# An inference step of a hybrid attention layer: the first weights' splits placed behind the key products, and one output weight split a stage later

## Chip, cores and metric

The kernel runs on one core of a Trainium2 chip. The metric is the device time in microseconds of one execution. A core has five engines that run side by side, each through its own program in order: TensorE (PE, matrix products; PEld is its loading of weights), VectorE (DVE), ScalarE (ACT), GpSimd (POOL) and SyncE (SP), which here issues the DMA transfers. They wait for each other on semaphores.

## The reference

One layer works on 512 prompt tokens and 64 sample tokens with a cache of 128 positions. A norm and one input projection feed two kinds of attention; their outputs go through one output projection, then through a gated feed-forward part with a short convolution and a last norm.

```
h = rmsnorm(x, g_attn)
proj = h @ w_in
q_d, k_d = rope(proj[..q..], pos), rope(proj[..k..], pos)      # differential heads
v_d = proj[..v..]
c_q, c_kv = rmsnorm(proj[..cq..], g_qa), rmsnorm(proj[..ckv..], g_kva)
k_r = rope(proj[..kr..], pos)                                  # latent heads' shared key
q_m = c_q @ w_qb;  kv = c_kv @ w_kvb
mix = concat(diff_attention(q_d, k_d, v_d), mla_attention(q_m, kv, k_r))
x1 = x + mix @ w_out
u, g = split(rmsnorm(x1, g_ffn) @ w_up)
y = x1 + (silu(causal_conv(g)) * u) @ w_down;  return rmsnorm(y, g_final), new keys, values, ...
```

## The kernel before

The 576 tokens (512 and 64) lie along the free side of the tiles, features along the 128 partitions. Columns are worked in two groups, 256 and 320 wide (GRP). A product in full precision is made of three matrix products of rounded halves: high by high, high by low, low by high (mm3, L140 to L142). So each weight tile must be split before its use: ScalarE copies the raw tile into its high half (split_hi, L126, rows named wv00h, wo0h), VectorE subtracts that from the raw one for the low half (split_lo, through tt, L84, rows named wv00l, wo0l). A weight of 1,024 columns is split in two parts of 512.

The order of work up to the feed-forward part is the order in which the program is written; it is made by generators that take steps beside each other. Two places matter here.

**The start.** TensorE makes the first pair of key products (kacc), then the first pair of query products (qacc, two halves of two column groups, 24 products each), then the values of the first heads (pv, function values, L440 to L443), then scores S (L500). Between each two inner steps of the query products, go advances two chains. first_chain does the first norm: norm_steps makes the root of the mean square for each token (r_col, GpSimd), waits ROW_STEPS steps, spreads it over the partitions (rbc, a transpose on TensorE, copied by ScalarE to r_bc, L331) and multiplies it into the rotary tables (cosr, sinr on VectorE). held_pair then multiplies the key products with the tables (pr, rope_evac, VectorE), sums them on GpSimd (st, rotate, through tt at L84 too) and stores them (store_pair, L393 and L395): eight stores of 32 rows bring the rotated rows into qkT. first_weights waits FIRST_WEIGHTS steps and then takes eight half splits, one at each step: high and low of both parts of wv00 and of wv01.

```
yield FIRST_WEIGHTS
for _ in range(8):
    filler.split()
    yield 1
```

**The filler.** Attention blocks alternate with projections that a Filler hands out in pieces. Its stages are, in order, V0, V1, ..., CQ, CKV, KR, QU, U0, U1, VM, ..., W0 (output projection). QU makes the latent queries (qracc, rotated sums q, split into qr) with the split of the shared key (kr, kro) and of the latent (lc into lat) beside it; U0 and U1 make the keys (knacc; knp, knl, kns) and queries (qnacc; qn, qnl, qns) of latent heads 0 and 1. wo0 is the first tile of the output weight. While a stage runs, its next weights are split, one half at every SPLIT_EVERY-th step, but only the weights that AHEAD lists for the stage; where it lists nothing, the weights of the next stage that has any:

```
if self.todo and self.todo[0][0] in self.ahead and self.count % SPLIT_EVERY.get(self.name, 1) == 0:
    self.split()
```

Loads of raw tiles go through SyncE's one queue, in order, with the stores; a raw buffer is loaded again when the split of the weight in it is done, so a load's place in the queue follows the split's place in the program.

Of the kernel before, what the change touches and what calls it, by code (L numbers as in the profile page):

```python
# [38 lines left out]

GAPS = ((1.0, 1.0, 1.0), (1.2, 1.2, 1.2), (0.8, 1.2, 1.2), (0.9, 0.9, 0.9), (0.8, 1.1, 1.1), (0.9, 1.0, 0.9))  # L40
NORM_STEPS = (3, 1, 4, 2)
LATE_STEPS, ROPE_STEPS, KEY_STEPS, ROW_STEPS, FIRST_WEIGHTS = 10, 2, 4, 3, 3
SPLIT_EVERY = {"V1": 3, "U1": 2, "CQ": 2, "KR": 2, "QU": 2, "U0": 2}
AHEAD = {"CQ": ("wi10", "wkr"), "CKV": ("wqr", "wqn"), "KR": ("wkv",), "QU": ("wo0",), "U0": ("wo0",)}
SQUARES_BEHIND, ADDS_BEHIND, NORM_BEGIN = 2, 3, 4
N2_FINISH, N2_SPREAD = 2, 4
Y_FINISH, Y_SPREAD, Y_CUTS = 1, 3, (0, 3, 6, 8)
# [18 lines left out]
def stream_step(ctx: ExitStack, tc: tile.TileContext, i, o):  # L66
# [887 lines left out]
    class Filler:  # L954
# [43 lines left out]
        def step(self):  # L998
# [4 lines left out]
            if self.gen is None:  # L1003
# [15 lines left out]
                self.ahead = self.loaded[first + len(specs):first + len(specs) + after]  # L1019
                if self.name in AHEAD:  # L1020
                    self.ahead = [w for w in self.loaded if w.name in AHEAD[self.name]]
                if self.name == "U1":
# [625 lines left out]
```

## Time and profile before

| | before |
|---|---|
| runs | 676.8, 675.14, 676.6 us; median 676.6 |
| profiled execution: own time | 676.81 us |
| its span in the trace | 674.9 us |
| granted TensorE clock, mean | 0.994 |
| TensorE busy | 656.8 us, 97% of the span, 4830 instructions |
| VectorE busy | 508.1 us, 75% |
| ScalarE busy | 313.8 us, 46% |
| GpSimd busy | 114.8 us, 17% |

The span is what the profile shows of the execution from its first to its last instruction; the execution's own time is 1.9 us longer. A busy share is a mean over the whole span and does not tell which engine a stage waits for; that is read from the rows' last column, in brackets, which gives an engine's idle time ahead of an instruction and who ended it.

### The profile page before, as it was taken

The page shows a single profiled execution, that of the slowest core. Times are in us where ns is not written, and L with a number is a line of the kernel's source. Part 1 is how long each engine was busy: PE and PEld are TensorE (multiplying, and loading weights), DVE is VectorE, ACT ScalarE, POOL GpSimd, SP SyncE. Part 2 cuts the span into 40 slices and gives each one's busy share as a digit, 9 for nine tenths or more (in the row PEclk, how much of TensorE's full clock was granted, in tenths as well). Part 3 has the DMA queues.
Part 4 walks back from the last instruction along what each step waited for, and adds up shares of the span by engine and source line. Part 5 has one row for each costly group of instructions (what it writes and reads, how often), then busy time and mean ns, then how long its engine had stood idle before and what let it go on. Part 6 is the DMA issues. An engine that isn't in the chain of part 4 may idle for free.

```text
span 674.9 us, 12335 instructions
## 1 busy us (share of the span) xinstructions
PE 656.8 (97%) x4830; PEld 631.5 (94%) x4830; DVE 508.1 (75%) x1022; ACT 313.8 (46%) x621; POOL 114.8 (17%) x166
## 2 busy tenths in 40 slices
PE   8999999998899999999999999999999999999995
PEld 8998897887799899999999999999999999999995
DVE  5758866778577757899999849984885788697634
ACT  8423335534634336375574236532641553464253
POOL 0131210015200016232230101210110010011042
PEclk9999999999999999999999999999999999999998
DMA  8464422225114113003133303330331133024103
GB/s 315 158 185 130 133 66 68 69 64 181 50 32 146 44 32 126 1 14 112 64 126 125 126 1 124 127 116 10 120 129 65 48 110 126 26 85 143 32 1 141
DMA packets 26249, 63.62 MB, mean 94 GB/s; under 512 B 3280, under 2 KB 6288, under 8 KB 26192
## 3 DMA queue, kind: packets, MB, share of 16 engines
q1 hardware_dynamic: 25904, 62.58, 28.3%
q8 instruction: 38, 0.62, 0.4%
q10 hardware_dynamic: 288, 0.26, 0.1%
q14 instruction: 19, 0.16, 0.1%
HBM read 55.27 MB, written 5.21 MB: 90 GB/s over the span
## 4 chain that ended last, share of the span: by engine, by line
PE 82%; DVE 10%; ACT 3%; issue 2%; DMA 1%; POOL 0%; SPq 0%; DVEq 0%; POOLq 0%; ACTq 0%
PE yacc L140 10%; PE yacc L141 9%; PE yacc L142 9%; PE ua L1265 6%; PE ua L1263 6%; PE ua L1264 6%; PE ub L1265 3%; PE ub L1264 3%; PE ub L1263 3%; PE uc L1265 2%; PE uc L1264 2%; PE uc L1263 2%; PE pv L440 2%; PE pv L441 1%; PE uplain L140 1%
## 5 line engine op out<-in xcount | busy, mean ns | idle before, releaser
L84 DVE TENSOR_TENSOR x<-x,yacc 128x288 f32<-128x288 f32 (+2 forms) x128 | 56.4, 449 | 48.8 <-PE yacc L142 48.5
L140 PE MATMUL yacc<-act,wd 128*128 128x288 f32 x288 | 85.2, 296 | 0.0
L142 PE MATMUL yacc<-act,wd 128*128 128x288 f32 x288 | 85.1, 296 | 0.0
L141 PE MATMUL yacc<-act,wd 128*128 128x288 f32 x288 | 85.1, 295 | 0.0
L141 PEld LDWEIGHTS yacc<-act,wd 128*128 128x128 f32 x288 | 54.3, 189 | 0.0
L142 PEld LDWEIGHTS yacc<-act,wd 128*128 128x128 f32 x288 | 54.3, 188 | 0.0
L140 PEld LDWEIGHTS yacc<-act,wd 128*128 128x128 f32 x288 | 54.3, 189 | 0.0
L1291 POOL COPY cst<-G 128x2 f32<-128x2 f32 x22 | 19.5, 889 | 163.7 <-DVE G L84 147.8
L468 ACT ACTIVATE p<-S,nmax 128x128 f32<-128x128 f32 (+4 forms) x36 | 18.5, 515 | 43.0 <-DVE nmax L466 42.6
L1352 ACT COPY u<-ua 128x288 f32<-128x288 f32 x20 | 8.0, 399 | 63.8 <-PE ua L1265 63.8
L87 DVE SCALAR_TENSOR_TENSOR conv<-G,vec,conv 128x578 f32<-128x578 f32 x44 | 35.8, 815 | 2.0 <-ACT conv L1296 1.9
L1278 POOL COPY G<-zero 128x2 f32<-128x2 f32 x22 | 14.4, 653 | 131.4 <-DVE conv L87 115.8
L84 POOL TENSOR_TENSOR n<-n,nsq 128x288 f32<-128x288 f32 x13 | 12.3, 950 | 75.5 <-ACT nsq L882 75.3
L1296 ACT ACTIVATE conv<-G,vec 128x578 f32<-128x578 f32 x22 | 19.2, 872 | 9.1 <-DVE G L84 9.0
L468 ACT ACTIVATE p<-Sm,nmax 128x128 f32<-128x128 f32 (+4 forms) x18 | 9.3, 515 | 28.5 <-DVE nmax L466 28.5
L84 POOL TENSOR_TENSOR st<-pr 128x256 f32<-128x256 f32 (+1 forms) x16 | 13.4, 858 | 50.0 <-DVE c L516 24.0
L90 ACT CAST act<-conv 128x576 fp32r<-128x576 f32 x22 | 14.9, 676 | 12.6 <-DVE conv L84 12.5
L1300 ACT ACTIVATE silu<-conv 128x578 f32<-128x578 f32 x22 | 15.1, 688 | 11.8 <-DVE conv L87 11.8
L480 DVE COPY pT<-tp 128x128 f32<-128x128 f32 (+3 forms) x36 | 16.6, 462 | 4.3 <-PE tp L477 3.8
L882 ACT ACTIVATE nsq<-x 128x288 f32<-128x288 f32 (+2 forms) x28 | 12.3, 443 | 16.1 <-DVE x L84 14.4
L477 PE MATMUL tp<-ident,p 128*128 128x128 f32 x84 | 15.6, 278 | 3.9 <-DVE p L795 1.3
L466 DVE TENSOR_REDUCE nmax<-S 128x1 f32<-128x128 f32 (+4 forms) x36 | 16.9, 475 | 1.1
(1585 smaller groups left out, 2536.9 us busy)
## 6 DMA issues: line engine op xcount, KB each, us to landing
qkT<-st SPq DMA_DIRECT2D x32, 72.0 KB, 2.0
xraw<-in_x SPq DMA_DIRECT2D x7, 288.0 KB, 5.8
x<-in_x SPq DMA_DIRECT2D x7, 288.0 KB, 5.9
out_y<-yo SPq DMA_DIRECT2D x4, 320.0 KB, 2.2
out_kd<-st SPq DMA_DIRECT2D x4, 288.0 KB, 2.4
out_vp<-vd SPq DMA_DIRECT2D x2, 512.0 KB, 4.2
wkr<-in_w_k SPq DMA_DIRECT2D x3, 256.0 KB, 5.4
out_y<-yo SPq DMA_DIRECT2D x2, 384.0 KB, 2.4
```

What stands on the lines that cost most here:

```text
L84: (eng or nc.vector).tensor_tensor(out=out, in0=a, in1=b, op=op)
L87: nc.vector.scalar_tensor_tensor(out=out, in0=a, scalar=s, in1=b, op0=op0, op1=op1)
L140: nc.tensor.matmul(out, lhsT=wh, rhs=xh, start=first, stop=False)
L141: nc.tensor.matmul(out, lhsT=wh, rhs=xl, start=False, stop=False)
L142: nc.tensor.matmul(out, lhsT=wl, rhs=xh, start=False, stop=last)
L466: nc.vector.tensor_reduce(out=nmax[:, 0:1], in_=Sv, axis=AX.X, op=ALU.max, negate=True)
L468: nc.scalar.activation(out=p[:, :nk], in_=Sv, func=AF.Exp, bias=nmax[:, 0:1], accum_out=sums)
L1263: nc.tensor.matmul(acc, lhsT=wh, rhs=xh, start=first and n == 0, stop=False, skip_group_check=True)
L1264: nc.tensor.matmul(acc, lhsT=wh, rhs=xl, start=False, stop=False, skip_group_check=True)
L1265: nc.tensor.matmul(acc, lhsT=wl, rhs=xh, start=False, stop=(n == len(ks) - 1), skip_group_check=True)
L1291: nc.gpsimd.tensor_copy(out=cst[:, j, 0:2], in_=G[:, 512:514])
L1296: nc.scalar.activation(out=c[:, :578], in_=G[:, 0:578], func=AF.Identity, scale=cw[0], bias=cb)
```

## The change

Four numbers change, all in the lines that set the order: the spreading of the norm's row begins after two steps instead of three, the first eight half splits after seven instead of three, and wo0 is no longer split during the stage QU. QU lists wkv, which is all split by then; U0 keeps wo0. The new entry for U1 names what U1 took by itself before.

```
-LATE_STEPS, ROPE_STEPS, KEY_STEPS, ROW_STEPS, FIRST_WEIGHTS = 10, 2, 4, 3, 3
+LATE_STEPS, ROPE_STEPS, KEY_STEPS, ROW_STEPS, FIRST_WEIGHTS = 10, 2, 4, 2, 7
 SPLIT_EVERY = {"V1": 3, "U1": 2, "CQ": 2, "KR": 2, "QU": 2, "U0": 2}
-AHEAD = {"CQ": ("wi10", "wkr"), "CKV": ("wqr", "wqn"), "KR": ("wkv",), "QU": ("wo0",), "U0": ("wo0",)}
+AHEAD = {"CQ": ("wi10", "wkr"), "CKV": ("wqr", "wqn"), "KR": ("wkv",), "QU": ("wkv",), "U0": ("wo0",), "U1": ("wkv", "wo0")}
```

On VectorE at the start, among the key products (pr from kacc) and the tables, the low halves of the first value weights move; a minus is a place of before, a plus one of the change:

```order
 L84 TENSOR_TENSOR pr<-kacc_128,cosr 128x256
 L84 TENSOR_TENSOR pr<-kacc_128,sinr 128x256
+L84 TENSOR_TENSOR wv00l<-wv00r,wv00h 128x512
 L84 TENSOR_TENSOR pr<-kacc_129,cosr 128x320
 L84 TENSOR_TENSOR pr<-kacc_129,sinr 128x320
 L84 TENSOR_TENSOR pr<-kacc_130,cosr 128x320
 L84 TENSOR_TENSOR pr<-kacc_130,sinr 128x320
-L84 TENSOR_TENSOR wv01l<-wv01r,wv01h 128x512
+L84 TENSOR_TENSOR wv00l<-wv00r,wv00h 128x512
+L84 TENSOR_TENSOR wv01l<-wv01r,wv01h 128x512 x2
```

Before, both halves of wv00l and the first of wv01l stood ahead of the tables; now one half of wv00l stands between the narrow and the wide key products, and the other three behind all of them. On TensorE the transposes rbc stand six products earlier, and ScalarE's four high halves stand behind its copies of r_bc.

On SyncE, in its queue of transfers behind the load of wi4, the first keys' stores (st to qkT, and to the output kd) change places with two loads:

```order
 L122 DMA wi4r<-in_w_in 128x512 x2
+L393 DMA qkT<-st_403 32x576 x4
+L395 DMA out_kd<-st_403 128x576
+L393 DMA qkT<-st_404 32x576 x4
+L395 DMA out_kd<-st_404 128x576
 L122 DMA wi5r<-in_w_in 128x512 x2
 L122 DMA wi6r<-in_w_in 128x512 x2
-L393 DMA qkT<-st_419 32x576 x4
```

The stores of the keys now come ahead of the loads of wi5 and wi6, which were ahead of them; the stores of the queries follow behind both, as before.

On VectorE in the stages QU and U0, around the queries' sums q and head 0's products, wo0's low halves move (the second one goes to the same place of head 1):

```order
 L87 SCALAR_TENSOR_TENSOR lc<-lc,vec,rbc 128x256
-L84 TENSOR_TENSOR wo0l<-wo0r,wo0h 128x512
 L84 TENSOR_TENSOR q<-pr 128x256
...
 L87 SCALAR_TENSOR_TENSOR pr<-qracc,msin 128x256
-L84 TENSOR_TENSOR wo0l<-wo0r,wo0h 128x512
 L84 TENSOR_TENSOR q<-pr 128x256
...
 L87 SCALAR_TENSOR_TENSOR qnl<-qnacc,qn 128x256 x2
+L84 TENSOR_TENSOR wo0l<-wo0r,wo0h 128x512
 L737 COPY kns<-knacc 128x192
```

Both low halves left QU: the first stands behind head 0's qnl, ahead of the copy kns, and the second between the two qnl of head 1. Their casts on ScalarE moved with them: the first now ahead of head 0's qn, the second ahead of head 1's knp.

## Rows read from the trace of the kernel before

**Rows 1.** TensorE's timeline, 31-37 us: start, busy us, engine, line, [idle <-releaser].
```profile
31.08 0.41 PE L140 MATMUL qacc<-xh,wq1h 128*128 128x320 f32 x1 [0.41 <-DVE pr L84]
31.33 0.31 PE L141 MATMUL qacc<-xl,wq1h 128*128 128x320 f32 x1
31.47 0.31 PE L142 MATMUL qacc<-xh,wq1l 128*128 128x320 f32 x1
...
36.97 0.28 PE L441 MATMUL pv<-wv01l,xh 128*128 128x256 f32 x1
```

**Rows 2.** VectorE's timeline, 28 to 37 us, same columns.
```profile
30.28 0.42 DVE L84 TENSOR_TENSOR pr<-kacc,cosr 128x256 f32<-128x256 f32 x1
...
32.53 0.49 DVE L84 TENSOR_TENSOR pr<-kacc,cosr 128x320 f32<-128x320 f32 x1 [0.85 <-POOL st L84]
...
34.13 0.68 DVE L84 TENSOR_TENSOR wv01l<-wv01r,wv01h 128x512 fp32r<-128x512 f32 x1
```

**Rows 3.** ScalarE's timeline, 27 to 29 us.
```profile
28.40 0.43 ACT L331 COPY r_bc<-rbc 128x320 f32<-128x320 f32 x1 [0.24 <-PE rbc L190]
```

**Rows 4.** GpSimd's timeline, 24 to 37 us.
```profile
31.76 1.43 POOL L84 TENSOR_TENSOR st<-pr 128x256 f32<-128x256 f32 x2 [5.93 <-DVE pr L84]
34.30 2.09 POOL L84 TENSOR_TENSOR st<-pr 128x320 f32<-128x320 f32 x2 [1.10 <-DVE pr L84]
```

**Rows 5.** SyncE's queue, 30 to 50 us; last, issues of 42 to 50.
```profile
34.84 0.81 SPq L122 DMA_DIRECT2D wi6r<-in_w_in  x2
35.69 2.50 SPq L393 DMA_DIRECT2D qkT<-st  x4
...
42.56 4.95 SPq L393 DMA_DIRECT2D qkT<-st  x8
...
qkT<-st SPq DMA_DIRECT2D x8, 72.0 KB, 2.1
```

**Rows 6.** TensorE's timeline, 48 us and 158 to 175 us.
```profile
48.22 0.49 PE L500 MATMUL S<-qkT 64*128 64x128 f32 x4
...
158.19 0.39 PE L140 MATMUL qracc<-lat,wqrh 128*128 128x256 f32 x1 [0.33 <-DVE pr L87]
...
163.19 0.50 PE L141 MATMUL knacc<-lat,wkvh 128*128 128x512 f32 x1 [1.32 <-DVE lat L84]
...
167.74 0.33 PE L477 MATMUL tp<-ident,p 128*128 128x128 f32 x1 [0.56 <-DVE p L87]
...
174.35 0.33 PE L477 MATMUL tp<-ident,p 128*128 128x128 f32 x1 [1.34 <-DVE p L795]
```

**Rows 7.** VectorE's timeline, 155 to 175 us.
```profile
156.00 1.39 DVE L84 TENSOR_TENSOR wo0l<-wo0r,wo0h 128x512 fp32r<-128x512 f32 x1
...
161.70 1.43 DVE L84 TENSOR_TENSOR lat<-lc,lat 128x576 fp32r<-128x576 f32 x1
...
166.13 0.42 DVE L87 SCALAR_TENSOR_TENSOR qnl<-qnacc,qn 128x256 fp32r<-128x256 f32 x1 [0.53 <-ACT qn L749]
...
170.19 0.74 DVE L87 SCALAR_TENSOR_TENSOR qnl<-qnacc,qn 128x256 fp32r<-128x256 f32 x2
```

**Rows 8.** ScalarE's timeline, 157 to 176 us.
```profile
157.56 0.61 ACT L126 CAST wo0h<-wo0r 128x512 fp32r<-128x512 f32 x1
...
159.72 0.78 ACT L694 CAST kr<-kr 64x704 fp32r<-64x704 f32 x1
...
170.96 0.22 ACT L752 ACTIVATE qns<-qnacc 128x64 f32<-128x64 f32 x1 [0.77 <-DVE qnl L87]
```

**Rows 9.** GpSimd's timeline, 148 to 195 us.
```profile
157.73 1.70 POOL L84 TENSOR_TENSOR kr<-kro,kr 64x704 fp32r<-64x704 f32 x1 [0.89 <-ACT kr L690]
161.22 2.09 POOL L84 TENSOR_TENSOR qr<-q,qr 64x512 fp32r<-64x512 f32 x2 [1.79 <-ACT qr L704]
165.77 1.70 POOL L84 TENSOR_TENSOR qr<-q,qr 64x512 fp32r<-64x512 f32 x2 [2.45 <-ACT qr L704]
```

**Rows 10.** Stretch of 2 us: engines' busy us, granted clock, DMA share, GB/s.
```profile
136.00:138.00 2.00, 2.00 (x11) 2.00 (x10) 0.00 (x0) 0.39 (x1) 0.00 (x0) 0.50 0.75 212
```

## The prediction

> **What bounds the kernel now.** I read the page's busy shares first, then the waits, then the timelines of the two stretches in which the change moves instructions. TensorE is busy for 97% of the span, so nothing off it counts unless it makes TensorE wait, and I look only at such waits. Around the first edit there is one: TensorE stands for 0.41 us at 31.08 because VectorE's first key products free their accumulator late [rows 1]. Its next matmuls follow each other by 0.14 us, but the first one holds its place for 0.25, so the stop costs about 0.5. Around the second edit there are three: 1.32 us at 163.19 for the low half of the latent, 0.56 at 167.74 and 1.34 at 174.35, both for a softmax row that VectorE finishes late [rows 6]. Behind each the chain is tight, so what makes one longer moves all that follows.
>
> The span of the profiled execution is 674.9 us and its own time 676.8, at the top of the three runs and 0.2 over their median. I sum against 676.8; about 2 us either way (0.3%) is all that a measurement can tell from no change.
>
> **First edit: tables ahead of the value weights' splits.** The transposes that spread the norm's row come out six matmuls earlier on TensorE: 6 x 0.14 = 0.9 us. In before, splits of value weights stand ahead of the table products on VectorE, the first key product starts at 30.28 [rows 2], and the second copy of the row waits for TensorE at 28.40 [rows 3]. With those transposes 0.9 earlier and no split between, the copy is done at about 28.40 + 0.43 - 0.9 = 27.9 and the second pair of tables can follow at once; four table products of about 0.37 then end near 29.0, and the first key product starts there instead of at 30.28, 1.25 earlier. TensorE's stop at 31.08 goes: **-0.5**.
>
> The three splits now come behind the key products, where GpSimd does the rotation's sums. There the rows show that the two engines do not work side by side on this kind of instruction: a low half takes VectorE 0.68 us at 34.13 [rows 2], but 1.39 at 156.00 [rows 7], while GpSimd sums the shared key; the latent's low half takes 1.43 at 161.70 [rows 7], under GpSimd's qr at 161.22 [rows 9]; and GpSimd's sums at 34.30 hold 2.09 us for two [rows 4], the first of them behind the split at 34.13. So I lay them end to end. Key products until 30.4, wv00l's half until 31.0, GpSimd's first two sums 31.0 to 32.4 (1.43, [rows 4]); VectorE's next product needs a buffer that the first of them frees, so it starts at about 31.8 (32.53 before) and four products of 0.40 end at 33.4. Then three splits of 0.6 and GpSimd's two wide sums, at 0.75 each a little over the narrow ones' 0.71, take turns: split to 34.05, sum to 34.8, split to 35.4, sum to 36.2, split to 36.9. TensorE wants that last half at 36.97 - 0.5 = 36.45 [rows 1]. It waits about 0.5: **+0.5**, and the gain of the first edit is given back. Bounds: if the splits all win their turn they are done by 35.3 and this is 0; if a sum also takes longer, 1.0.
>
> The Trainium skill, page "SBUF — State Buffer", section "SBUF: two separate sides", says that VectorE and GpSimd share a pair of ports under an exclusive lock that whoever starts first holds for a whole instruction. The 1.39 us in place of 0.68 agrees; by the page alone, without durations, one could not tell who starts first.
>
> **The queue of stores.** SyncE's list moves too. The rotated keys' stores now stand ahead of the loads of wi5 and wi6 instead of behind them. In before they start at 35.69, after the pair wi6r (0.81 from 34.84) [rows 5]; now they can start when the sums are done, and the two pairs of loads, 2 x 0.85 = 1.7 us of issuing, lie between them and the queries' stores. From the first key store to the first query store the queue needs 42.56 - 35.69 = 6.87 us, so with the first key store at 34.85 the queries' start at 34.85 + 6.87 + 1.7 = 43.4, 0.85 later. Head 0's scores need six of the eight stores: issued at 42.56 + 5/8 x 4.95 = 45.65, landed 2.1 later [rows 5], 47.75. TensorE starts those scores at 48.22 and comes to their second half at about 48.45, so 0.7 us of margin goes against 0.85 of delay: **+0.2** (0 if the sums let the keys go earlier still, 0.6 if the keys' sums end with the split at 36.2).
>
> A page puts this otherwise. The Trainium skill, "DMA: Bandwidth & Descriptors", section "Issuing engines are not separate DMA queues", calls the issuing engine's share usually small beside the transfer; by it this term would be 0 and the sum 0.2 less. The row shows 4.95 us for eight issues and 2.1 to the landing, so here the issue is the larger.
>
> **Second edit: wo0's split leaves the query stage.** It takes away two low halves on VectorE and two casts on ScalarE ahead of 163.19. Three things hold what that is worth. The half at 156.00 stood behind GpSimd anyway; the product behind it will stand there too. GpSimd's kr runs from 157.73 to 159.43 [rows 9], and VectorE's sum q(320) waits for it as before. And ScalarE's copy of kr at 159.72 [rows 8] can start only 0.25 earlier, at GpSimd's end, so GpSimd's qr comes 0.25 earlier too, at about 161.0; the latent's low half, freed of the second wo0l (0.6), is due at 161.1 and finds GpSimd there, as it does at 161.70 now. Latent 0.3 earlier: **-0.3**. Bounds: 0, and the whole 1.32 if VectorE gets in first; the two arrive 0.1 us apart, and I take the side of the rows, on which GpSimd leads.
>
> In its new place the first cast (0.61, [rows 8]) stands ahead of ScalarE's qn, and with it qnl's second half at 166.13 comes about 0.35 late. Behind it wo0l's first half is due at 166.9 less the 0.3, while GpSimd's qr (two, 1.70 us from 165.77) [rows 9], itself 0.4 later with the cast, holds it up for another 0.6; then it needs 0.6. The copy of the keys and the softmax scaling stand behind it on VectorE, and TensorE's transpose at 167.74 waits for them: 0.35 + 0.6 + 0.6 = **+1.5**. Bounds: 0.6, the half alone; 2.0, cast and the contended half of 1.39.
>
> The second cast goes ahead of head 1's knp, 0.5 after overlap, and its low half between the two qnl at 170.19 [rows 7], 0.6. ScalarE's qns at 170.96 waits for the second qnl (0.77 already) [rows 8], and the squares, qr, knp, VectorE's knl and the transpose at 174.35 stand behind in that order: 0.5 + 0.6 = **+1.1**. GpSimd is idle there, so no contention. Bounds: 0.6 if ScalarE's idle time before qn takes the cast; 1.1.
>
> Sum: -0.5 + 0.5 + 0.2 - 0.3 + 1.5 + 1.1 = +2.5; 676.8 + 2.5 = **679.3**.
>
> **The rivals.** *A, main:* 679.3, 0.4% over the median. *B, the clock:* behind a longer standstill TensorE's clock falls; in before a stretch of 2 us runs at 0.50, 1.2 GHz [rows 10], which loses 1.0 us. For it: the wait at 174.35 grows to 2.4. Against: the 1.32 and 1.34 of now leave no such stretch. 680.3. (The Trainium skill's "TensorE: Matmul & The Clock Gate", section "What's actually happening", describes a gate that lets half the pulses through when the array is not busy.) *C, the port is free:* VectorE's latent half gets in ahead of GpSimd (-1.3 for -0.3), or wo0l's first half meets no GpSimd (+0.9 for +1.5); one of them gives 678.3 to 678.7, both 677.7. That is no measurable change. For it: the two arrivals are 0.1 apart. I take 678.2. *D, nothing:* the splits land in gaps on all sides and the first gain is given back: 676.8. For it: VectorE is idle 0.53 ahead of 166.13 [rows 7]. Against: the casts use up just that gap. *E, faster:* wo0's low halves lay on TensorE's path in the query stage and lie off it in their new place. Then the wait of 1.32 at 163.19 goes whole, with it the 0.33 at 158.19 behind the contended first half [rows 6], and the 0.5 at 31.08 stays won: -2.1, 674.7. It decides at the latent's half, if that is done by 161.7, and at the transpose, if that is 1.6 earlier than 167.74. Against it stands the order on VectorE, where wo0l sits directly ahead of the softmax scaling.
>
> **How the numbers follow.** Chances: A 0.42, B 0.13, C 0.22, D 0.13, E 0.10. The likeliest is 679.3. The terms all at their lower bounds add to -0.6, 676.2, all at their upper ones to +4.2, 681.0. The range reaches down half way from D to E and up to just past B: 675.6 to 680.8. Over 678.6 counts as slower, under 674.6 as faster: slower is A and B less their lower edge, 0.50; faster E, 0.10; the same C, D and that edge, 0.40.
>
> **What would show it.** In the changed kernel's trace: no stop of TensorE ahead of the wide query products near 31; wv01l's last half at 36 to 37, interleaved with GpSimd's sums, and a wait of 0.3 to 0.7 in the first value products; query stores from about 43.4, and a wait ahead of the first scores; a wait at the latent still over 1 us near 163; wo0l's first half 1.2 to 1.4 us long near 166.6; transposes at about 169 and 176.5. It is wrong if the latent's half is done before 162 and the first wo0l takes 0.7, or if the two splits do not lie on the chain to the transposes; then the time is at 678 or below. A clock of 0.50 near 175 would point to B.

## The result and the profile after

The changed kernel takes 681.89 us (median of 4 runs, 680.67 to 682.85) against 676.36 (4 runs, 675.14 to 676.8): a ratio of 1.0087, 95% interval 1.0075 to 1.0099. It is slower, as forecast, but by 5.5 us and not 2.5, and it lies above the range.

| | before | after |
|---|---|---|
| profiled execution: own time, span | 676.81, 674.9 | 681.38, 679.5 |
| TensorE busy | 656.8 us | 658.2 us |
| VectorE busy | 508.1 us | 511.1 us |
| granted TensorE clock, mean | 0.994 | 0.990 |

I laid TensorE's instructions of both profiles side by side and read where the start of the same instruction shifts. First, rows of TensorE's timeline after, which answer to [rows 1, 6] (columns as there; in brackets at the end, the idle time ahead and who ended it):

```profile
30.54 0.31 PE L140 MATMUL qacc<-xh,wq1h 128*128 128x320 f32 x1
30.68 0.31 PE L141 MATMUL qacc<-xl,wq1h 128*128 128x320 f32 x1
...
36.53 0.38 PE L441 MATMUL pv<-wv01l,xh 128*128 128x256 f32 x1
36.75 0.28 PE L443 MATMUL pv<-wv01h,xl 128*128 128x256 f32 x1
...
50.63 0.68 PE L500 MATMUL S<-qkT 64*128 64x128 f32 x4 [2.63 <-DMA qkT<-st]
...
165.47 0.50 PE L141 MATMUL knacc<-lat,wkvh 128*128 128x512 f32 x1 [1.35 <-DVE lat L84]
...
171.28 0.33 PE L477 MATMUL tp<-ident,p 128*128 128x128 f32 x1 [1.82 <-DVE p L87]
...
179.06 0.33 PE L477 MATMUL tp<-ident,p 128*128 128x128 f32 x1 [0.98 <-DVE p L795]
```

The stop at 31.08 is gone: the same product starts at 30.54 with no idle time ahead of it, and the one behind it at 30.68 for 31.33, while the products ahead of the stop start within 0.03 us of before's: 0.7 won. The last half of wv01l, now at 36.53, costs 0.3: the product behind it starts at 36.75 for 37.10, only 0.35 earlier. Then the first scores, which started at 48.22, start at 50.63, after 2.63 us of waiting for the stores of the rotated queries. The latent's wait is 1.35, as before (1.32). The transposes wait 1.82 (0.56 before) and 0.98 (1.34). Next, SyncE's queue after, with the issues of 42 to 51 us behind it, to set beside [rows 5]:

```profile
34.67 2.50 SPq L393 DMA_DIRECT2D qkT<-st  x4
...
41.05 0.91 SPq L122 DMA_DIRECT2D wi5r<-in_w_in  x2
...
42.95 0.43 SPq L1100 DMA_DIRECT2D msin<-in_msin  x1
43.48 6.63 SPq L393 DMA_DIRECT2D qkT<-st  x8
...
qkT<-st SPq DMA_DIRECT2D x8, 72.0 KB, 4.9
```

The queries' stores start at 43.48, where the prediction had 43.4. But they take 6.63 us to issue (4.95 before), and from issue to landing 4.9 (2.1 before; both are medians of the eight). Ahead of them in the queue stand the loads of wi5, wi6 and msin: four tiles of 256 KB and one of 288 KB, issued within two and a half microseconds. Two single issues, msin and the first query store, with their time to landing, and the waits of SyncE's queue from 40.5 to 50.3 us (who waited for what: us in total, times, longest) tell more:

```profile
msin<-in_msin SPq DMA_DIRECT2D x1, 288.0 KB, 6.6
qkT<-st SPq DMA_DIRECT2D x1, 72.0 KB, 6.3
...
SPq L393 <- DMA wi6r<-in_w_in: 1.2, 2, 0.7
SPq L393 <- DMA msin<-in_msin: 0.8, 1, 0.8
```

Issued at 42.95 and 43.48, the two landed at 49.6 and 49.8: the first store came in right behind msin, and the next four 0.2 us apart, the fifth at 50.6, where TensorE's wait ends. These five were issued at the pace of before (3.06 us). The sixth to eighth were not: each was issued only when the transfer eight places ahead of it in the queue, wi6's first half, its second half and msin, had landed. That is how 4.95 became 6.63; it follows from the late landings and does not cause them. The clock, in stretches of 2 us (columns as in [rows 10]):

```profile
52.00:54.00 2.00, 2.00 (x12) 2.00 (x12) 0.97 (x3) 2.00 (x7) 0.00 (x0) 0.52 0.98 300
54.00:56.00 2.00, 2.00 (x13) 2.00 (x13) 0.43 (x2) 0.12 (x1) 0.00 (x0) 0.62 0.97 348
...
136.00:138.00 2.00, 2.00 (x21) 1.99 (x19) 1.75 (x5) 1.78 (x6) 0.66 (x2) 1.00 0.00 0
...
172.00:174.00 2.00, 2.00 (x10) 2.00 (x10) 0.76 (x2) 1.49 (x5) 0.00 (x0) 0.50 0.00 0
```

Behind the 2.63 us in which TensorE stood, the granted clock falls to the 1.2 GHz level (0.52 and 0.62 of 2.4 GHz are means of two stretches that hold some time at the full clock); behind the 1.82 us at the transpose it is 0.50. The stretch at 136, which ran at 0.50 in before [rows 10], runs at full clock. The shifts in this pair of profiles are then:

| place | predicted | measured |
|---|---|---|
| stop near 31 | -0.5 | -0.7 |
| late splits of wv00, wv01 | +0.5 | +0.3 |
| first scores, for the query stores | +0.2 | +2.8 |
| half clock behind them | 0 | +1.5 |
| half clock near 135, there in before only | 0 | -1.6 |
| query stage without wo0, read at the latent | -0.3 | -0.3 |
| first transpose | +1.5 | +1.3 |
| second transpose (from the first one to it) | +1.1 | +1.2 |

They add to 4.5 of the 4.6 us between the two profiled executions; two smaller shifts, -0.3 at a transpose near 59 us and +0.3 at one near 141, cancel.

### The profile page after: what moved, and what is told of

Same layout as the page of the kernel before. It is cut to its first block, busy times and chain, and to the rows that moved or that the text cites. A ratio compares the mean times of both kernels' runs of the same rounds, so it can differ in the third digit from the quotient of the medians.

```text
span 679.5 us, 12335 instructions
## 1 busy us (share of the span) xinstructions
PE 658.2 (97%) x4830; PEld 632.9 (93%) x4830; DVE 511.1 (75%) x1022; ACT 313.6 (46%) x621; POOL 115.8 (17%) x166
## 4 chain that ended last, share of the span: by engine, by line
PE 82%; DVE 9%; ACT 3%; issue 2%; DMA 1%; SPq 1%; POOL 1%; DVEq 0%; POOLq 0%; ACTq 0%
PE yacc L140 9%; PE yacc L141 9%; PE yacc L142 9%; PE ua L1265 6%; PE ua L1264 6%; PE ua L1263 6%; PE ub L1265 3%; PE ub L1264 3%; PE ub L1263 3%; PE uc L1265 2%; PE uc L1264 2%; PE uc L1263 2%; PE uplain L140 1%; PE tp L477 1%; PE uplain L142 1%
## 5 line engine op out<-in xcount | busy, mean ns | idle before, releaser
L477 PEld LDWEIGHTS tp<-ident,p 128*128 128x128 f32 x84 | 10.1, 140 | 8.5 <-issue 2.7
```

Source lines behind the costliest of these rows:

```text
L477: nc.tensor.transpose(out=pt_ps[:, n * P:n * P + P], in_=a[:, c:c + P], identity=ident)
```

## The experiments

Theory 1: the loads that now stand ahead of the query stores delay them as transfers, by their bytes, and not by the time that their issue takes. Rivals: the issue is what counts, as the prediction had it; the sums on GpSimd make the stores late; the loss comes from the second edit. Each kernel ran with the kernel before on the same chip; ratios are against that.

| run | what differs | median us | before us | ratio, 95% interval |
|---|---|---|---|---|
| e1_first | first edit alone | 679.39 | 676.43 | 1.0050 (1.0035 to 1.0064) |
| e2_second | second edit alone | 678.71 | 676.43 | 1.0041 (1.0026 to 1.0055) |
| e3_rows | row steps alone | 676.18 | 676.43 | 0.9994 (0.9983 to 1.0006) |
| e4_hold | change, wi6 and msin behind the stores | 680.27 | 676.43 | 1.0065 (1.0050 to 1.0080) |
| e5_behind | second edit, halves at other places of U0 | 677.22 | 676.92 | 1.0005 (0.9997 to 1.0013) |
| e6_u1 | second edit, split in U1 | 680.43 | 676.92 | 1.0060 (1.0048 to 1.0072) |
| e7_msin | row steps, msin behind the stores | 676.36 | 676.92 | 0.9996 (0.9988 to 1.0005) |
| e8_both | e7 and e5 together | 676.01 | 676.92 | 0.9987 (0.9979 to 0.9995) |
| e9_issue | e4 with three tiny transfers added | 681.23 | 677.10 | 1.0067 (1.0050 to 1.0084) |

**The first edit alone.** AHEAD as before:

```
-LATE_STEPS, ROPE_STEPS, KEY_STEPS, ROW_STEPS, FIRST_WEIGHTS = 10, 2, 4, 3, 3
+LATE_STEPS, ROPE_STEPS, KEY_STEPS, ROW_STEPS, FIRST_WEIGHTS = 10, 2, 4, 2, 7
```

> The first edit alone (row steps 2, first weights 7; wo0 split in its old place). Theory 1 (the loads of wi5 and wi6, 1 MB, and the 288 KB of msin stand ahead of the query stores as transfers, and these land late): TensorE waits 2.5 to 2.9 us ahead of the first scores, then runs some 3 us at half clock (1.5), less 0.5 for the stop near 31: +3.8, or +2.1 if the half-clock stretch near 135 us of before goes away as it did with both edits: 678.5 to 680.2. Rival (the prediction's own terms: only the issuing of the loads counts): +0.2, 676.6. Rival 2 (the loss comes from the second edit alone): 675.9.

It costs 3.0 us. TensorE's row for the first scores:

```profile
50.98 0.74 PE L500 MATMUL S<-qkT 64*128 64x128 f32 x4 [2.09 <-DMA qkT<-st]
```

The wait for the stores is there without the second edit; their median time to landing is 4.5 us. The two edits alone cost 3.0 and 2.3, together 5.3 of the 5.5: they add. The prediction's 0.2 for the first is refuted, and so is a loss in the second alone.

**The second edit alone.** The line of step counts as before, AHEAD as in the change.

> The second edit alone (wo0 split in U0 and not in QU). Theory 1: the first scores start as in before; the transpose of head 0 comes 1.0 later in balance (-0.4, +1.4) and a stretch of half clock behind it costs 1.5: +2.1 to +2.5, 678.5 to 678.9, with wo0l's first half at 1.1 to 1.4 us. Rival (the half clock behind the transpose comes only with the late start): +1, 677.4. Rival 2 (the loss is all in the first edit): 676.4.

TensorE's rows for the two transposes:

```profile
167.81 0.33 PE L477 MATMUL tp<-ident,p 128*128 128x128 f32 x1 [1.82 <-DVE p L87]
...
175.60 0.33 PE L477 MATMUL tp<-ident,p 128*128 128x128 f32 x1 [0.99 <-DVE p L795]
```

The same waits as in the changed kernel, with the first scores on time. So +2.3 is the second edit's own, within 0.1 of the sum of its three predicted terms (-0.3 + 1.5 + 1.1). The rival that half clock here needs the late start falls too: the granted clock is 0.56 to 0.59 from 168 to 172 us.

**Row steps alone.** This sends the key stores ahead of wi6's load only.

```
-LATE_STEPS, ROPE_STEPS, KEY_STEPS, ROW_STEPS, FIRST_WEIGHTS = 10, 2, 4, 3, 3
+LATE_STEPS, ROPE_STEPS, KEY_STEPS, ROW_STEPS, FIRST_WEIGHTS = 10, 2, 4, 2, 3
```

> Row steps 2 alone: the tables start earlier, first weights stay at 3; of the loads only wi6's pair and msin now stand between the key stores and the query stores. Theory 1: half the dose, the query stores land 0.7 to 1.5 later than in before and the first scores wait 0 to 0.8; with the stop near 31 gone: -0.5 to +0.3, 675.9 to 676.7, and no half clock at 51. Rival (any load between the stores costs the full wait): +2.3 or more, 678.7.

Its queue, the first scores and the stores' landing:

```profile
40.95 0.89 SPq L122 DMA_DIRECT2D wi6r<-in_w_in  x2
...
42.42 4.95 SPq L393 DMA_DIRECT2D qkT<-st  x8
...
47.84 0.62 PE L500 MATMUL S<-qkT 64*128 64x128 f32 x4 [0.29 <-DMA qkT<-st]
...
qkT<-st SPq DMA_DIRECT2D x8, 72.0 KB, 3.1
```

With one of the two pairs of loads ahead of the stores their landing takes 3.1 us, between 2.1 and 4.9; the wait is 0.29. The stop near 31 goes here too. The time does not differ measurably from before.

**The loads held.** The changed kernel, with wi6 and msin issued behind the query stores:

```
 for part in range(n // 512):
-    w.load(part) if n > 512 else None
+    if name in ('wi6',):
+        self.held.append((w, part))
+    elif n > 512:
+        w.load(part)
...
-nc.sync.dma_start(out=msin, in_=i["msin"])
...
 drain(held_pair(qacc, False))
+for w, part in filler.held:
+    w.load(part)
+nc.sync.dma_start(out=msin, in_=i["msin"])
```

> The changed kernel with the load of wi6 and that of msin issued behind the query stores; nothing else moves. Theory 1: the stores start near 42.2 instead of 43.5, land in time or up to 0.7 late, and the wait of 2.63 ahead of the first scores shrinks below 0.8, with no half clock at 52 to 55: 4 us back, or 2.3 if the stretch of half clock near 135 returns: 677.9 to 679.6. Rival (the sums on GpSimd or the splits make the stores late, not the loads): 681.9.

Its rows of the same views, with the first row of TensorE that waits in this stretch:

```profile
40.71 0.90 SPq L122 DMA_DIRECT2D wi5r<-in_w_in  x2
41.70 4.95 SPq L393 DMA_DIRECT2D qkT<-st  x8
...
46.35 0.39 PE L440 MATMUL pv<-wv00h,xs 128*128 128x256 f32 x1 [0.66 <-ACT vd L448]
...
qkT<-st SPq DMA_DIRECT2D x8, 72.0 KB, 2.3
```

The stores land 2.3 us after their issue, and the wait ahead of the first scores is gone, half clock with it. That is theory 1; the sums and the splits are where they were. The time fell only to 680.3, above what I expected. In the profiled run the half clock near 135 is back, as in before, and two new waits came: 0.66 here, for values that ScalarE evacuates behind its cast of wi5, whose load landed late, and 0.71 at a transpose near 60, where wi6, now loaded later, holds up VectorE's splits.

**Issues without bytes.** The kernel with the loads held, with three transfers of 2 KB in their place:

```
+for n in range(3):
+    few = sb.tile([P, 4], F32, tag="few", bufs=3, name=f"few{n}")
+    nc.sync.dma_start(out=few, in_=i["lam"][:, 4 * n:4 * n + 4])
 drain(held_pair(qacc, False))
```

> The kernel with the loads of wi6 and msin behind the query stores, and in their former place three transfers of 2 KB each into a tile that nothing reads (extra work, the output is the same): the queue issues as many transfers ahead of the query stores as in the changed kernel, but 0.8 MB fewer bytes. Theory 1 (the bytes): the stores start near 43, land 2.1 to 2.6 us after their issue, and the first scores wait 0 to 0.9; time 0 to 1 over the run with the loads held, 680.3 to 681.3. Rival (the issuing, or the later start, is what costs): the landing takes over 4 us and the wait is 2 or more, as in the changed kernel.

```profile
41.83 1.38 SPq L1107 DMA_DIRECT2D few<-in_lam  x3
43.31 4.95 SPq L393 DMA_DIRECT2D qkT<-st  x8
...
48.58 0.46 PE L500 MATMUL S<-qkT 64*128 64x128 f32 x2 [0.18 <-issue]
...
170.03 0.33 PE L477 MATMUL tp<-ident,p 128*128 128x128 f32 x1 [1.82 <-DVE p L87]
...
177.76 0.33 PE L477 MATMUL tp<-ident,p 128*128 128x128 f32 x1 [2.02 <-DVE p L795]
...
qkT<-st SPq DMA_DIRECT2D x8, 72.0 KB, 2.0
```

This is the run that separates the theories. The stores start at 43.31, within 0.2 of the changed kernel, behind as many issues; without 0.8 MB of loads ahead they issue in 4.95 and land in 2.0 us. TensorE waits 0.2 between the halves of the scores; with the gap ahead of it the delay there is 0.8, not 2.8. So of the 2.8 lost, about 0.8 goes with the issue and the later start, and about 2.0 with the bytes. The Trainium skill, "DMA: Bandwidth & Descriptors", section "Issuing engines are not separate DMA queues", says that transfers share the same 16 engines whoever issues them and that the issue is usually the small part. The prediction set that sentence aside for the row's 4.95 us of issue; by the two runs the transfer is the larger part here, as the sentence has it. The term of 0 that the prediction read out of it is no nearer to the 2.8 than its own 0.2. The run's time is no better than with the loads held, because wi6's late landing costs more at the transposes behind (1.39 near 56).

**The first half behind the scaling.** Second edit alone, with

```
-SPLIT_EVERY = {"V1": 3, "U1": 2, "CQ": 2, "KR": 2, "QU": 2, "U0": 2}
+SPLIT_EVERY = {"V1": 3, "U1": 2, "CQ": 2, "KR": 2, "QU": 2, "U0": 3}
```

> The second edit alone, with wo0's halves at every third step of U0 instead of every second: the first low half now stands behind the softmax scaling of head 0 and its maximum, no longer ahead of them and of GpSimd's qr; the second one behind both qnl of head 1. Theory 1 (the first low half ahead of the scaling, held up by GpSimd, made the transpose late, and that wait brought the half clock): the wait at the transpose falls from 1.82 to 0.6 to 1.0, no half clock behind it, -0.5 to +0.4: 675.9 to 676.8. Rival (the casts on ScalarE are what makes it late, wherever the low half stands): a transpose wait of 1.4 or more and 678.5, as with the second edit alone.

VectorE's second qnl of head 0 and wo0l, and TensorE's transpose:

```profile
165.38 0.43 DVE L87 SCALAR_TENSOR_TENSOR qnl<-qnacc,qn 128x256 fp32r<-128x256 f32 x1 [1.07 <-ACT qn L749]
...
167.30 0.68 DVE L84 TENSOR_TENSOR wo0l<-wo0r,wo0h 128x512 fp32r<-128x512 f32 x1
...
166.99 0.33 PE L477 MATMUL tp<-ident,p 128*128 128x128 f32 x1 [1.10 <-DVE p L87]
```

The low half takes 0.68 here, clear of GpSimd, and the transpose's wait falls from 1.82 to 1.10. The cast ahead of qn keeps the rest: VectorE waits 1.07 for ScalarE's qn, 0.53 in before [rows 7]. No half clock follows, and 2.0 of the second edit's 2.3 us are back (1.0005 for 1.0041). They have two sources, because the edit moves the second half too, behind both qnl of head 1: the first transpose comes 0.5 later and not 1.3, and the second one behind it 0.1 later and not 1.2. Both parts of the predicted +1.5, the cast and the half held up by GpSimd, are seen.

**All of wo0 in U1.** AHEAD with "U0": ("wkv",).

> The second edit with U0 listing wkv instead of wo0, so that all of wo0 is split in U1: the first half now stands where the second one stood (cast ahead of head 1's knp, low half between its two qnl), the second half behind kns. Theory 1: the transpose of head 0 is on time and TensorE keeps the 0.4 won in QU; the transpose of head 1 comes 1.1 later by the first half (hidden behind half clock so far) and up to 0.6 more by the second: +0.7 to +1.3 without a half clock, 677.1 to 677.7, or 679 with one. Rival (there is room in U1): 675.9.

```profile
167.59 0.33 PE L477 MATMUL tp<-ident,p 128*128 128x128 f32 x1 [0.57 <-DVE p L87]
...
175.85 0.47 PE L477 MATMUL tp<-ident,p 128*128 128x128 f32 x1 [2.56 <-DVE p L795]
...
173.73 0.69 DVE L84 TENSOR_TENSOR wo0l<-wo0r,wo0h 128x512 fp32r<-128x512 f32 x1 [1.56 <-ACT wo0h L126]
```

The first transpose is as before (0.57), so what made it late was the first half alone. The second one waits 2.56, for a chain in which ScalarE's second cast now stands too, and half clock (0.50 from 176 to 178 us) follows, which costs 1.4 more. At 3.5 us it costs more than I expected; there is no room in U1.

**msin behind the stores.** Row steps alone, and the load of msin moved behind drain(held_pair(qacc, False)).

> Row steps 2 alone, with the load of msin (288 KB) issued behind the query stores instead of ahead of them. Theory 1 (bytes ahead of the stores make them land late): the wait of 0.29 ahead of the first scores goes, the median time from issue to landing of the query stores falls from 3.1 to about 2.6 us: -0.8 to -1.2 against the kernel before, 675.2 to 675.6. Rival (only the pair of wi6 or the late start counts): no more than row steps alone, 676.1.

The stores land in 2.3 us instead of 3.1 and the scores wait no more, as theory 1 has it; but the time is 0.9996 of before (0.9988 to 1.0005), where a gain of 0.8 us or more, 0.9988 or less, was expected. The gain at the scores is 0.3 us, below what 12 runs resolve.

**What is left of both.** Row steps 2, msin behind the stores, AHEAD of the change and "U0": 3.

> Row steps 2, msin behind the query stores, and wo0's halves out of QU at every third step of U0: what is left of both edits without their two costs. Theory 1: the sum of the two runs beside it, -0.8 to -1.2 and -0.5 to +0.4: -1.7 to -0.4, 674.7 to 676.0. Rival (the gains are eaten by the stretches of half clock that come with another spacing): 676.5 or more.

At 0.9987 (0.9979 to 0.9995) it is the only version that beats the kernel before, by 0.9 us, inside the 0.4 to 1.7 that were expected.

**Both kernels once more.**

> The kernel before, profiled once more. Theory 1 as far as it says that the stretch of half clock near 135 us comes by chance from one execution to the next: it may be absent or of another length here, with all waits of TensorE the same as in the first profile. Rival (it belongs to the kernel): the same 1.7 us at the same place.

> The changed kernel, profiled once more. Theory 1: again the wait of 2.6 us ahead of the first scores and 1.8 at the transpose, each with half clock behind it; near 135 either. Rival: other waits.

Their times are 676.94 and 680.88 us. The changed kernel's waits, and its stores' landing:

```profile
47.54 0.38 PE L440 MATMUL pv<-wv00h,xs 128*128 128x256 f32 x1 [0.83 <-ACT vd L448]
...
51.36 0.68 PE L500 MATMUL S<-qkT 64*128 64x128 f32 x4 [1.64 <-DMA qkT<-st]
...
qkT<-st SPq DMA_DIRECT2D x8, 72.0 KB, 4.9
```

The stores land late again, by the same 4.9 us. This time the standstill comes in two parts, 0.83 at the values and 1.64 at the scores, and together they shift TensorE by the same 2.8; my expectation of 2.6 in one piece was wrong. And no half clock follows: this is the stretch behind the scores in that run, 0.52 in the first profile.

```profile
52.00:54.00 2.00, 2.00 (x18) 2.00 (x18) 0.89 (x5) 1.60 (x6) 0.00 (x0) 1.00 0.87 262
```

Near 135 the second profile of before runs at half clock again, so I could not show with it that this comes by chance. But the second edit alone, e5 and e6 have the same program up to there, and e5 has none while the other two and both profiles of before do. The stretch from 136 to 138 us, first in before_again, then in e5_behind:

```profile
136.00:138.00 2.00, 2.00 (x10) 2.00 (x10) 0.19 (x1) 0.69 (x1) 0.00 (x0) 0.50 0.77 211
```

```profile
136.00:138.00 2.00, 2.00 (x16) 1.47 (x13) 0.69 (x2) 0.69 (x1) 0.00 (x0) 1.00 0.51 167
```

## Why the prediction was wrong

**The tables and the late splits.** Right: the stop went (-0.7 for -0.5), and the splits alternate with GpSimd's sums, which shows in VectorE's row of two halves at 2.65 us for 1.3 and in GpSimd's wide sums at 2.54:

```profile
31.62 0.49 DVE L84 TENSOR_TENSOR pr<-kacc,cosr 128x320 f32<-128x320 f32 x1 [0.63 <-POOL st L84]
...
33.23 0.68 DVE L84 TENSOR_TENSOR wv00l<-wv00r,wv00h 128x512 fp32r<-128x512 f32 x1
33.83 2.65 DVE L84 TENSOR_TENSOR wv01l<-wv01r,wv01h 128x512 fp32r<-128x512 f32 x2
```

```profile
33.39 2.54 POOL L84 TENSOR_TENSOR st<-pr 128x320 f32<-128x320 f32 x2 [1.10 <-DVE pr L84]
```

The key product starts at 31.62 (31.8 predicted), the three splits and two wide sums lie between 33.23 and 36.48, and TensorE lost 0.3 at the last half, not 0.5. End to end is right: at the prediction's own 0.6 for a split and 0.75 for a sum they take 3.3 us, and 3.25 were measured. Its list of times from 33.4 to 36.9 holds 3.5, so 0.2 of the +0.5 is a slip of adding.

**The queue of stores.** This is the step that failed: "landed 2.1 later". I moved the stores' start by the issue of the four loads, correctly to 0.1 us, and kept the row's landing time of before, although that row was measured with only msin just ahead of the stores. The 1 MB that I had just moved into their way I costed by its issue alone. The term was +0.2, its upper bound 0.6; it measured +2.8. The runs order the median landing by the loads just ahead: 2.1 us with msin alone (before), 2.0 with wi5 and three transfers of 2 KB behind it, 2.3 with wi5 or wi6, 3.1 with wi6 and msin, 4.9 with wi5, wi6 and msin. And in every one of these profiles the first query store landed 0.2 us behind the transfer ahead of it in the queue: at 45.40 behind msin's 45.22 in before, at 49.78 behind 49.59 after, at 45.34 behind the last 2 KB's 45.14 in e9_issue. So the stores' landing followed that of the loads, and not their own issue. The issue alone was nearly right: TensorE came to the scores 0.4 earlier than the prediction had it (-0.7 + 0.3 for -0.5 + 0.5), which makes its +0.2 a +0.6, and e9_issue measured +0.8.

**wo0 out of QU.** Right in place and size. GpSimd's qr still gets in ahead of the latent's low half, by 0.26 us, the latent comes 0.3 earlier, and its wait stays. TensorE's 0.33 at 158.19 [rows 6] went too, but TensorE then waited for the latent all the same.

```profile
163.79 1.62 DVE L84 TENSOR_TENSOR lat<-lc,lat 128x576 fp32r<-128x576 f32 x1
...
163.53 2.06 POOL L84 TENSOR_TENSOR qr<-q,qr 64x512 fp32r<-64x512 f32 x2 [1.53 <-ACT qr L704]
```

**wo0 in U0.** Right: the first low half takes 1.13 while GpSimd's qr runs (2.01 us from 168.34), and the first transpose shifts by 1.3 (1.5 predicted). The second comes 1.2 later behind the first (1.1 predicted).

```profile
169.04 1.13 DVE L84 TENSOR_TENSOR wo0l<-wo0r,wo0h 128x512 fp32r<-128x512 f32 x1
...
168.34 2.01 POOL L84 TENSOR_TENSOR qr<-q,qr 64x512 fp32r<-64x512 f32 x2 [2.75 <-ACT qr L704]
```

**The clock.** Rival B has the clock fall behind a longer standstill. The stretch that it cites, near 135 in before, has none ahead of it: from 118 us on TensorE has no idle time of 0.15 us or more. Half clock behind the transpose was rival B's place, and it came there, but it costs nothing: in e9_issue the clock stays at 1.00 behind a first transpose of the same wait, and the second transpose still comes 7.73 us after the first, against 7.78 with half clock and 6.61 in before. e9_issue's stretch, for the 0.50 of the changed kernel:

```profile
170.00:172.00 2.00, 1.97 (x15) 1.98 (x16) 0.39 (x3) 1.49 (x5) 0.00 (x0) 1.00 0.00 0
```

The chain on VectorE and ScalarE sets the time of the second transpose, and TensorE merely waits less at its end (0.98 for 2.02). Behind the scores half clock cost 1.5 in the first profile and did not come in the second; near 135 it differs between runs of the same program up to there. So the clock moves single executions by 1.5 us. What decides it in one and not in the other stays open.

In sum, the second edit was forecast at +2.3 and measured +2.3; the first at +0.2 and measured +3.0. Its three terms add to +2.4 in the changed kernel's rows (-0.7, +0.3, +2.8), and the error is in one of them: the stores' landing, 2.6 too small. I can't place the other 0.6; a stretch of half clock that comes in one execution and not in the next is larger than that.

## What to carry to other kernels

When an edit moves loads ahead of a store or load that someone waits for, cost the bytes that will be in flight as well as the issue: a time to landing read in the old order holds only for what stood ahead of it there. A split that is moved for one engine's sake moves the reload of its buffer in the queue; look there first, at what is due next. And a piece of work that is short on its engine can cost its full length, and the wait for another engine with it, when it is put directly ahead of the instruction that TensorE waits for (here 1.13 us for a half of 0.68).

## What I had not expected of the hardware

The stores' issue itself grew, from 4.95 to 6.63 us for the same eight, when 1.3 MB stood ahead of them, and fell back to 4.95 when the bytes were gone at the same number of issues: three of the eight issues waited, 2.0 us in all, for the landing of the transfer eight places ahead. Why eight, no row here shows. The granted clock near 135 and behind the first scores was not the same in executions of equal program and nearly equal waits. And half clock behind a wait was free where another engine's chain set the next wait, and cost 1.4 us where none did (e6_u1).
